# A bidirectional mLSTM encoder: an early mask, forward k weighted on ScalarE and VectorE, and another order of the pools

## The chip, the core and the metric

One core of a Trainium2 chip runs the whole kernel. The metric is the device time of one execution in microseconds (us), the median of the runs. The engines are TensorE (PE in the profile; PEld is its weight load), VectorE (DVE), ScalarE (ACT), GpSimd (POOL), and the queue SP, whose engine issues nearly all DMAs in order.

## The reference: what is computed

Two sequences, a prompt of 2048 tokens and a sample of 256, go through two layers: windowed attention, then a bidirectional mLSTM, each with gates and a residual, and a final RMS norm. All data is float32, width 1024. The change touches the mLSTM layer only, of 4 heads with 128 elements of q and k and 256 of v. Cut to what matters:

```python
def mlstm_chunkwise(q, k, v, ig, fg):
...
    logf = jax.nn.log_sigmoid(fg...)
    b = jnp.cumsum(logf, axis=-1)
    D = jnp.where(tri, b[..., :, None] - b[..., None, :] + igc[..., None, :], -jnp.inf)
    a = b_end[..., None] - b + igc
    m_loc = jnp.max(a, axis=-1)
    w = jnp.exp(a - m_loc[..., None])
    C_loc = jnp.einsum('bhcsk,bhcsv->bhckv', w[..., None] * kc, vc)
...
    def step(carry, inp):
        C, n, m = carry
        C_l, n_l, m_l, be = inp
        m_new = jnp.maximum(be + m, m_l)
        sp = jnp.exp(be + m - m_new)
        sl = jnp.exp(m_l - m_new)
        C_new = sp[..., None, None] * C + sl[..., None, None] * C_l
...
    P = jnp.exp(D - m_t[..., None]) * jnp.einsum('bhctk,bhcsk->bhcts', qc, kc)
    num = jnp.einsum('bhcts,bhcsv->bhctv', P, vc) + sc[..., None] * jnp.einsum('bhctk,bhckv->bhctv', qc, Cs)
    h = num / jnp.maximum(jnp.abs(den), jnp.exp(-m_t))[..., None]

def mlstm_mixer(xn, w_in, gate_bias, head_norm, w_out):
...
    h = h_f + h_b
    h = h * lax.rsqrt(jnp.mean(h * h, axis=-1, keepdims=True) + EPS)
...
    h = h * jax.nn.sigmoid(o) * jax.nn.silu(z)
    return h @ w_out
```

So a state C, 128 x 256 a head, runs forward over the chunks, and a second one backward; each chunk's output needs both.

## The kernel before, in words

The tokens lie in 18 tiles of 128, 16 of the prompt (one segment) and 2 of the sample (the other). Float32 products are made from parts: an operand is split into a high part (xhi, whi, kh, vh: a cast on ScalarE) and a low part (xlo, wlo, kl, v: a subtraction on VectorE), and three products, high x high, low x high and high x low, are summed in PSUM. The big projections go over pairs of tiles as Winograd products: seven products of half matrices instead of eight, lines 293 to 295, in the PSUM tiles pj, c and d. Lines 342 to 344 are a plain product of the first pair of a stage, lines 398 to 400 the last projection.

The mLSTM layer comes in four stages.

1. `mlstm_qkv` projects q, k, v and the gates' inputs and stores them in DRAM.
2. `gate_sums` turns the gates' inputs into scales for each tile and head. It is one serial chain of small steps: sums over a tile (pb, pe), a transpose (pu, uT), its maximum (um), a product that puts 72 maxima on one partition (pr, umr), then on VectorE the scan over the 18 tiles in both directions (lines 763 and 766, names rw, umr, be; each step needs the one before), an exponential (spr), products that spread the results to all partitions (pl), the weights of k (line 777), a scan within the tiles (msc, MT), and rows (nT, sT) that are stored in DRAM for later; em at line 797 is the last exponential. Its tiles are in the pool "gt".
3. `mlstm_gates_states` projects z and o, Winograd over nine pairs and two column halves. `use` (lines 866 to 880) takes a PSUM tile, adds the Winograd sum u where there is one (tile s), applies the Sigmoid into a tile e (line 872), multiplies (lines 874, 879) and stores to `go`. Meanwhile the backward state runs: `back_state` stores C to `Cb` and `state_update` makes cu products (line 828) from the parts of the weighted k and of v. The tiles e and s are in the pool "b2", k, v and C in "b2s".
4. `mlstm_core` runs forward. Generators for a tile are interleaved after the string ORDER: `weights` loads q, k (both transposed), rows and v, and makes E, the masked and exponentiated decay matrix times S = k q (S at line 919, mask cm added at line 926, exp at 928, times S at 929, parts Eh and El), and qs, the scaled q (line 933, on GpSimd); `core` makes num (line 948 from E and v, line 950 from the states and qs), the quotient hh, its sum of squares ss and the norm (lines 961 to 966); `update` weights k and updates the forward C; `back` transposes hh, splits it and projects it with w_mo (lines 398 to 400), and the final norm is stored to y.

What sets the order. Tile's scheduler lists the instructions of each engine ahead of time, and each engine then runs its list in order. Pools are opened and closed as the stages go, and a tile of a new pool waits for those tiles that held its bytes before. Raw loads from DRAM go through rings of slots: "rawx", "raww" (8 slots) and, in stage 3, "rawk".

In the compiled program the pools lie as follows (bytes in each partition). Before, b2 comes first: its three e and two s are at 126816 to 137056, which stage 2 does not use; b2s follows with kl, kh, v, vh and C at 137056 to 153536. The tiles of gate_sums are at 145120 to 155424. In the core, b3v's v parts are at 130912 to 139168.

The forward k's weighting is `weighted_k` (line 811): a raw load, one multiplication on GpSimd (line 817), a cast on ScalarE (818) and a subtraction on VectorE (819). The mask is loaded at the start of the core (line 894), the weights w_mo ahead of the loop over the tiles.

Of the kernel before, what the change touches and what calls it, by code (L numbers as in the profile page):

```python
# [11 lines left out]
F32 = mybir.dt.float32  # L12
F32R = mybir.dt.float32r
BF16 = mybir.dt.bfloat16
AF = mybir.ActivationFunctionType
ALU = mybir.AluOpType
# [4 lines left out]
D = 1024  # L21
# [6 lines left out]
MH, DQK, DV = 4, 128, 256  # L28
# [17 lines left out]
AORDER = "fffssssfsffffppsvppv"  # L46
AORDER1 = "fffssssfsffffppsvppv"
AORDER2 = "ssppsspvpv"
KX, WL = 0, 0
PH3, PL3 = (), ()  # L50
EA, ES, EQ = 2, 18, 0
ORDER = "cubwbubccucbcbuwubbbbbbw"
# [3 lines left out]
def seg_of(t):  # L56
    for s in SEGS:
        if s[0] <= t < s[1]:
            return s


class Trunk:
# [748 lines left out]
    def weighted_k(self, p, t, d, raw=()):  # L811

        nc = self.nc
        k = self.stage(self.k[t][:].rearrange("p h d -> p (h d)"), *raw).rearrange("p (h d) -> p h d", h=MH)
        lo = p.tile([128, MH, DQK], F32R, tag="kl", name="kl", bufs=1)
        hi = p.tile([128, MH, DQK], F32R, tag="kh", name="kh", bufs=1)
        nc.gpsimd.tensor_mul(k, k, self.w[:, d, t, :].unsqueeze(2).to_broadcast([128, MH, DQK]))
        nc.scalar.copy(hi[:], k)
        nc.vector.tensor_sub(lo[:], k, hi[:].bitcast(F32))
        return hi, lo  # L820
# [14 lines left out]
    def mlstm_gates_states(self):  # L835
        nc, tc, a = self.nc, self.tc, self.a
        with ExitStack() as st:
            pe = st.enter_context(tc.tile_pool(name="b2", bufs=2, reuse_waits="tile"))
            p = st.enter_context(tc.tile_pool(name="b2s", bufs=1, reuse_waits="tile"))
            ps = st.enter_context(tc.tile_pool(name="b2ps", bufs=1, space=PSUM, reuse_waits="tile"))  # L840
            prev = None

            ready = {}

            def operands(t):
                if t > 0 and t > seg_of(t)[0]:
                    ready[t] = self.weighted_k(p, t, 1, ("rawk",)), self.parts(p, self.v[t], "v", raw=("rawk",))

            def back_state(t):
                nonlocal prev  # L850
                s0, s1 = seg_of(t)
                if t < s1 - 1:
                    nc.sync.dma_start(self.Cb[t][:], prev[:])
                if t > s0:
                    if t == s1 - 1:
                        prev = p.tile([128, MH, VW], F32, tag="C", name="C", bufs=1)
                    self.state_update(ps, 1, t, *ready.pop(t), prev, prev, t == s1 - 1)
                operands(t - 1)

            operands(NT - 1)  # L860
            X = None
            for b in range(2):

                part = {}

                def use(t, h, o, u, b=b):
                    if u is not None:
                        s = pe.tile([128, 512], F32, tag="s", name="s", bufs=2)[:]
                        nc.vector.tensor_add(s, o, u)
                        o = s  # L870
                    e = pe.tile([128, 512], F32, tag="e", name="e", bufs=3)[:]
                    nc.scalar.activation(e, o, AF.Sigmoid)
                    if h == 0:
                        (nc.vector if u is None else nc.gpsimd).tensor_mul(e, e, o)  # L874
                    if t not in part:
                        part[t] = e
                        return
                    o = part.pop(t)
                    nc.gpsimd.tensor_mul(e, e, o)
                    nc.sync.dma_start(self.go[t][:, b * 512:(b + 1) * 512], e)  # L880

                X = self.winograd_pass(self.xn2T, a["w_oz"], b * 1024, self.g[:, 1], use, lambda n, pair: back_state(NT - 1 - b * len(PAIRS) - n),
                                       self.xn2T[:2] if b == 0 else None, X, True)


    def mlstm_core(self, y):
        nc, tc, a = self.nc, self.tc, self.a
        with ExitStack() as st:
            pool = lambda n, **k: st.enter_context(tc.tile_pool(name=n, bufs=2, reuse_waits="tile", **k))
            TRP, TRT = self.sps, "s"  # L890
            py, pm, pv, p, pe = pool("b3y", side="right"), pool("b3m"), pool("b3v"), pool("b3"), self.early
            ps = pool("b3ps", space=PSUM)
            cm = py.tile([128, 2, 128], F32, tag="cm", name="cm", bufs=1)
            nc.sync.dma_start(cm[:], a["causal"])
            w = []
            fg = pm.tile([128, D], F32, tag="fg", name="fg", bufs=1)
            nc.sync.dma_start(fg[:], a["final_g"].to_broadcast([128, D]))
            state = {0: None}
            W, H, R = {}, {}, {}

# [69 lines left out]
            def update(t):  # L970
                s0, s1 = seg_of(t)
                if t == s1 - 1:
                    state[t + 1] = None
                    return
                kw = self.weighted_k(py, t, 0, () if t < KX else ("raww",))
                yield
                C = p.tile([128, MH, VW], F32, tag="C", name="C", bufs=2)
                state[t + 1] = C
                for h in range(MH):
                    self.state_update(ps, 0, t, kw, W[t][3], state[t], C, t == s0, [h], 1)  # L980
                    yield

            def back(t):
                hh = H[t][:].rearrange("p h d -> p (h d)")
                xs = []
                for b in range(2):
                    tp = TRP.tile([128, 4, 128], F32, tag=TRT, name="tr", bufs=1)
                    for j in range(4):
                        nc.tensor.transpose(tp[:, j, :], hh[:, (b * 4 + j) * 128:(b * 4 + j + 1) * 128], self.ident[:])
                    xs += self.split(tp[:].rearrange("p c q -> p (c q)"))  # L990
                    yield
                x = [p.tile([128, 512], F32, tag="x", name="x", bufs=3)[:] for b in range(2)]
                for b in range(2):
                    nc.sync.dma_start(x[b], self.x2[t][:, b * 512:(b + 1) * 512])
                for b in range(2):
                    po = self.pj()
                    for qt in range(4):
                        self.project(po, xs, w[b], range(qt * 2, qt * 2 + 2))
                        if qt == 3:
                            nc.vector.tensor_add(x[b], x[b], po[:])  # L1000
                        yield
                rs = p.tile([128, 1], F32, tag="rs", name="rs", bufs=2)
                self.rms(p, x, rs[:])
                for b in range(2):
                    cols = slice(b * 512, (b + 1) * 512)
                    nc.vector.scalar_tensor_tensor(x[b], x[b], rs[:], fg[:, cols], ALU.mult, ALU.mult)
                    nc.sync.dma_start(y[t * 128:(t + 1) * 128, cols], x[b])
                yield

            self.free = deque(x for x in self.free if x[0] is self.wp)  # L1010
            for _ in weights(0):
                pass
            if not WL:
                w += self.load_w(a["w_mo"], [[512]] * 2, self.g[:, 2], PH3, PL3)
            for t in range(NT + 1):
                gens = {"c": core(t) if t < NT else iter(()), "u": update(t) if t < NT else iter(()),
                        "b": back(t - 1) if t > 0 else iter(()), "w": weights(t + 1) if t + 1 < NT else iter(())}
                for i, k in enumerate(ORDER):
                    if t == 0 and i == WL and WL:
                        w += self.load_w(a["w_mo"], [[512]] * 2, self.g[:, 2], PH3, PL3)  # L1020
                    next(gens[k], None)
                for g in gens.values():
                    for _ in g:
                        pass

    def run(self, y):
        nc, tc, a, ctx = self.nc, self.tc, self.a, self.ctx
        pjp = ctx.enter_context(tc.tile_pool(name="pjp", bufs=2, space=PSUM))
        self.pj = lambda: pjp.tile([128, 512], F32, tag="pj", name="pj")
        with tc.tile_pool(name="wy", bufs=1, side="right") as wy:  # L1030
# [3 lines left out]
            with ExitStack() as st:  # L1034
                right = lambda n, **k: st.enter_context(tc.tile_pool(name=n, bufs=1, side="right", reuse_waits="tile", **k))
# [9 lines left out]
                with tc.tile_pool(name="gps", bufs=1, space=PSUM, reuse_waits="tile") as self.gps:  # L1045
                    self.mlstm_qkv(first)
                    self.gate_sums()
                self.early = ctx.enter_context(tc.tile_pool(name="b3e", bufs=2, reuse_waits="tile"))
                self.mlstm_gates_states()
            self.xring = kept  # L1050
        self.mlstm_core(y)
# [81 lines left out]
```

## Time and profile before

| | |
|---|---|
| median of 3 runs (lowest, highest) | 2306.89 us (2303.06, 2307.14) |
| the profiled execution, its own time | 2307.11 us |
| its span on the core | 2305.0 us |
| mean granted TensorE clock in the span | 0.986 |
| busy: TensorE, weight loads, VectorE | 2217.8, 1763.9, 1505.6 us |
| busy: ScalarE, GpSimd | 1136.4, 464.1 us |

The times in the views are microseconds from the span's start. Stage 3's plain product ends at 1515.2, its last Winograd product at 1886.5; the core takes the rest. A row of a timeline has the start, the length, the engine, the line, the operation with its output and inputs, the shapes, how many instructions it stands for, and in brackets how long the engine was idle before it and what ended that. Matmuls overlap: one of 512 columns is listed with 0.39 us, but the next starts 0.23 us later. A row of groups has the busy time of all, the mean of one in ns, and the idle time ahead of them.

### The profile page before, as it was taken

How to read it: one execution, taken by the hardware profiler on the slowest of the kernel's cores; microseconds unless marked ns; L12 is line 12 of the kernel's file. 1: busy time of each engine (PE TensorE's matmuls, PEld its weight loads, DVE VectorE, ACT ScalarE, POOL GpSimd, SP SyncE). 2: the span in 40 equal slices, each digit the busy share in tenths (PEclk: the TensorE clock that was granted, in tenths of full speed). 3: DMA queues.
4: the chain of work that ended last, by engine and by line, in shares of the span. 5: the costliest groups of instructions: out<-in, count | busy, mean ns of one | idle time of the engine just before them, and what ended most of it. 6: DMA issues, size and time to landing. Idle time of an engine off the chain costs nothing. (4 is left out here: it accounts for less than half of the span.)

```text
span 2305.0 us, 33121 instructions
## 1 busy us (share of the span) xinstructions
PE 2217.8 (96%) x11102; PEld 1763.9 (77%) x11102; DVE 1505.6 (65%) x3303; ACT 1136.4 (49%) x2565; POOL 464.1 (20%) x392
## 2 busy tenths in 40 slices
PE   8999999999899999999999999999999977999998
PEld 7767676767567887788788899978878866888887
DVE  7565656565887779668656422386697576777784
ACT  6454545454764335557534411365464455454453
POOL 3211121211001222332000000022232243333320
PEclk9999999999999999999999999999999997999999
DMA  7111111111225447657655622356576565665641
GB/s 266 48 39 49 39 48 39 49 38 40 92 65 197 150 159 237 214 197 267 217 175 183 228 92 92 124 197 196 187 252 211 182 229 194 203 195 197 210 161 69
DMA packets 181802, 347.40 MB, mean 151 GB/s; under 512 B 20064, under 2 KB 22912, under 8 KB 181632
## 3 DMA queue, kind: packets, MB, share of 16 engines
q1 hardware_dynamic: 181488, 345.27, 45.0%
q8 instruction: 88, 1.44, 0.3%
q14 instruction: 82, 0.67, 0.1%
q10 hardware_dynamic: 144, 0.01, 0.0%
HBM read 247.93 MB, written 97.28 MB: 150 GB/s over the span
## 5 line engine op out<-in xcount | busy, mean ns | idle before, releaser
L398 PE MATMUL pj<-whi,xhi 128*128 128x512 f32 (+2 forms) x1152 | 433.6, 377 | 9.1 <-ACT whi L168 5.6
L123 ACT CAST xhi<-rawx 128x512 fp32r<-128x512 f32 x372 | 228.5, 618 | 418.4 <-PE pj L399 108.5
L400 PE MATMUL pj<-whi,xlo 128*128 128x512 f32 (+2 forms) x1152 | 423.2, 372 | 8.3 <-DVE xlo L124 8.3
L399 PE MATMUL pj<-wlo,xhi 128*128 128x512 f32 (+2 forms) x1152 | 426.3, 370 | 0.0
L124 DVE TENSOR_TENSOR xlo<-rawx,xhi 128x512 fp32r<-128x512 f32 x338 | 249.5, 743 | 106.7 <-ACT xhi L123 94.9
L400 PEld LDWEIGHTS pj<-whi,xlo 128*128 128x128 f32 x1152 | 218.0, 189 | 52.3 <-DVE xlo L124 11.4
L398 PEld LDWEIGHTS pj<-whi,xhi 128*128 128x128 f32 x1152 | 217.7, 189 | 51.3 <-issue 8.8
L399 PEld LDWEIGHTS pj<-wlo,xhi 128*128 128x128 f32 x1152 | 217.9, 189 | 36.6 <-issue 2.4
L536 ACT ACTIVATE Sm<-Sm,nm 128x384 f32<-128x384 f32 (+1 forms) x288 | 167.0, 581 | 95.0 <-DVE nm L530 88.6
L293 PE MATMUL pj<-whi,xhi 128*128 128x512 f32 x480 | 192.4, 401 | 2.7 <-DVE e L874 1.3
L294 PE MATMUL pj<-wlo,xhi 128*128 128x512 f32 x480 | 191.5, 399 | 0.4 <-DVE wlo L191 0.4
L295 PE MATMUL pj<-whi,xlo 128*128 128x512 f32 x480 | 191.3, 399 | 0.0
L525 DVE CUSTOM_DVE_ANT_0 Sm<-s,mask 128x384 f32<-128x384 f32 (+1 forms) x272 | 136.0, 530 | 72.1 <-PE s L523 69.0
L549 PE MATMUL ptp<-ident,Sm 128*128 128x128 f32 x800 | 135.3, 280 | 9.8 <-DVE PT L552 6.4
L549 PEld LDWEIGHTS ptp<-ident,Sm 128*128 128x128 f32 x800 | 94.6, 141 | 54.3 <-ACT Sm L536 19.0
L293 PE MATMUL c<-whi,xhi 128*128 128x512 f32 x320 | 127.5, 399 | 2.9 <-ACT whi L190 2.9
L293 PE MATMUL d<-whi,xhi 128*128 128x512 f32 x320 | 128.1, 400 | 1.4 <-DVE x L640 1.4
L294 PE MATMUL c<-wlo,xhi 128*128 128x512 f32 x320 | 127.1, 397 | 0.7 <-DVE wlo L191 0.7
L295 PE MATMUL c<-whi,xlo 128*128 128x512 f32 x320 | 127.0, 397 | 0.0
L294 PE MATMUL d<-wlo,xhi 128*128 128x512 f32 x320 | 126.4, 395 | 0.0
L295 PE MATMUL d<-whi,xlo 128*128 128x512 f32 x320 | 126.3, 395 | 0.0
L522 PE MATMUL s<-KH,Q 128*128 128x384 f32 (+1 forms) x288 | 106.0, 379 | 10.2 <-DVE mx L525 4.6
(242 smaller groups left out, 4650.9 us busy)
## 6 DMA issues: line engine op xcount, KB each, us to landing
rawx<-xn2T SPq DMA_DIRECT2D x128, 256.0 KB, 3.6
x<-x SPq DMA_DIRECT2D x108, 256.0 KB, 3.9
rawx<-xT SPq DMA_DIRECT2D x72, 256.0 KB, 3.0
raww<-w_oz SPq DMA_DIRECT2D x64, 256.0 KB, 4.8
rawx<-xsum SPq DMA_DIRECT2D x64, 256.0 KB, 3.0
raww<-w_qkvg SPq DMA_DIRECT2D x40, 256.0 KB, 4.3
v<-v SPq DMA_DIRECT2D x18, 516.0 KB, 3.8
rawx<-v SPq DMA_DIRECT2D x36, 258.0 KB, 2.8
```

Source lines behind the costliest of these rows:

```text
L123: nc.scalar.copy(hi[:], src)
L124: (eng or nc.vector).tensor_sub(lo[:], src, hi[:].bitcast(F32))
L293: nc.tensor.matmul(o, xh, wh, start=i == 0 and not more, stop=False, skip_group_check=more)
L294: nc.tensor.matmul(o, xh, wl, start=False, stop=False, skip_group_check=more)
L295: nc.tensor.matmul(o, xl, wh, start=False, stop=i == 3, skip_group_check=more)
L398: nc.tensor.matmul(o[:, :n], xh, wh, start=kt == 0, stop=False)
L399: nc.tensor.matmul(o[:, :n], xh, wl, start=False, stop=False)
L400: nc.tensor.matmul(o[:, :n], xl, wh, start=False, stop=kt == KT - 1)
L522: nc.tensor.matmul(S[:, :nk, :], q, KH[:, g, win, :], start=True, stop=False)
L525: nc.vector.tensor_tensor_reduce(Sm[:, :nk], S[:, :nk], mask[:, t % 3, win, :], 1.0, MASKED, ALU.add, ALU.max, mx[:, c:c + 1])
L536: nc.scalar.activation(Sg[c][:, :nk], Sg[c][:, :nk], AF.Exp, bias=nm[:, c:c + 1], scale=HD ** -0.5, accum_out=rs[:, c:c + 1])
L549: nc.tensor.transpose(tp[:, c, :], Ss[g][c][:, j, :], self.ident[:])
```

## The change

Four edits, in words:

1. The mask cm is a tile of the pool "b3e" (`self.early`), which is open over stages 3 and 4, and its load is issued ahead of `mlstm_gates_states`.
2. `weighted_k` for the forward direction (d == 0) has, for each of the four heads, a copy with a scale on ScalarE into the high part and a fused multiply and subtract on VectorE into the low one. GpSimd does nothing there. Its raw loads have a ring of their own, two slots taken from raww's eight. The switch KX, which was 0, is gone.
3. The pools are opened in another order: b2s before b2 in stage 3, b3v before b3m in the core, and the x tiles move from "b3" to "b3m". In the compiled program b2s is then at 127840 to 144320, e at 144320 to 150464 and s at 150464 to 154560, and the core's v parts are at 127840 to 144352, on the bytes of b2s.
4. w_mo is loaded inside the loop, at tile 0, and `issue_after` puts what ScalarE does for it behind the last Sigmoid of stage 3; the load of final_g follows it.

```diff
-KX, WL = 0, 0
+WL = 0
...
+        if d == 0:
+            for h in range(MH):
+                wk = self.w[:, d, t, h:h + 1]
+                nc.scalar.activation(hi[:, h], k[:, h], AF.Copy, scale=wk)
+                nc.vector.scalar_tensor_tensor(lo[:, h], k[:, h], wk, hi[:, h].bitcast(F32), ALU.mult, ALU.subtract)
+            return hi, lo
...
+            p = st.enter_context(tc.tile_pool(name="b2s", bufs=1, reuse_waits="tile"))
             pe = st.enter_context(tc.tile_pool(name="b2", bufs=2, reuse_waits="tile"))
-            p = st.enter_context(tc.tile_pool(name="b2s", bufs=1, reuse_waits="tile"))
...
-                    nc.scalar.activation(e, o, AF.Sigmoid)
+                    self.gated = nc.scalar.activation(e, o, AF.Sigmoid)
...
-            py, pm, pv, p, pe = pool("b3y", side="right"), pool("b3m"), pool("b3v"), pool("b3"), self.early
+            py, pv, pm, p, pe = pool("b3y", side="right"), pool("b3v"), pool("b3m"), pool("b3"), self.early
...
-            cm = py.tile([128, 2, 128], F32, tag="cm", name="cm", bufs=1)
-            nc.sync.dma_start(cm[:], a["causal"])
+            cm = self.cm
             w = []
+            ring = self.rings["raww"]
+            self.rings["rawk"] = deque(ring.pop() for _ in range(2))
...
-                kw = self.weighted_k(py, t, 0, () if t < KX else ("raww",))
+                kw = self.weighted_k(py, t, 0, ("rawk",))
...
-                x = [p.tile([128, 512], F32, tag="x", name="x", bufs=3)[:] for b in range(2)]
+                x = [pm.tile([128, 512], F32, tag="x", name="x", bufs=3)[:] for b in range(2)]
...
-            if not WL:
-                w += self.load_w(a["w_mo"], [[512]] * 2, self.g[:, 2], PH3, PL3)
...
-                    if t == 0 and i == WL and WL:
-                        w += self.load_w(a["w_mo"], [[512]] * 2, self.g[:, 2], PH3, PL3)
+                    if t == 0 and i == WL:
+
+                        with tc.issue_after(self.gated.ins):
+                            w += self.load_w(a["w_mo"], [[512]] * 2, self.g[:, 2], PH3, PL3)
+                        nc.sync.dma_start(fg[:], a["final_g"].to_broadcast([128, D]))
...
+                self.cm = self.early.tile([128, 2, 128], F32, tag="cm", name="cm", bufs=1)
+                nc.sync.dma_start(self.cm[:], a["causal"])
                 self.mlstm_gates_states()
```

Lines behind `weighted_k` have numbers that are six higher in the changed kernel (872 is 878 there, 919 is 925, 948 is 954).

The edits move instructions. TensorE where stage 2 ends and stage 3 begins, before: the last products of the plain pair (c, lines 342 to 344), then the first of the Winograd pair (pj, lines 293 to 295).

```order
L342 MATMUL c<-whi,xhi 128x512
L343 MATMUL c<-wlo,xhi 128x512
L344 MATMUL c<-whi,xlo 128x512
L293 MATMUL pj<-whi,xhi 128x512
L294 MATMUL pj<-wlo,xhi 128x512
L295 MATMUL pj<-whi,xlo 128x512
```

The same place in the changed kernel. s is the core's S of tile 0; pr, pl, pm and pM belong to gate_sums, cu to the backward state, of which only the first three of nine are shown (they differ in no name from the rest).

```order
L344 MATMUL c<-whi,xlo 128x512
L925 MATMUL s<-qT,kT 128x128 x4
L750 MATMUL pr<-ident,um 1x72 x2
L775 MATMUL pl_15014<-rw,ones 128x144
L772 MATMUL pl<-spr,ones 128x144
L782 MATMUL pm<-ones,rw 72x1 x2
L795 MATMUL pM<-ident,MT 128x72 x2
L834 MATMUL cu<-vh,kh 128x258
L834 MATMUL cu<-v,kh 128x258
L834 MATMUL cu<-vh,kl 128x258
...
L293 MATMUL pj<-whi,xhi 128x512
```

All of gate_sums' products after pu, which before stand among the Winograd products, now stand ahead of the first of them, and so do nine cu products and tile 0's S.

ScalarE at the same place in the changed kernel: spr, the weights of k (line 777), the rows (sT), em (line 797), a copy of the backward state's first C, and then the first Sigmoids (line 878), on the plain pair's pj.

```order
L770 ACTIVATE spr<-spr 1x144
L777 ACTIVATE scr<-scr 128x144
L790 ACTIVATE sT<-MT,msc 72x128
L824 CAST kh<-rawk 128x512
L790 ACTIVATE sT<-MT,msc 72x128
L797 ACTIVATE scr<-scr 128x144
L836 COPY C<-cu 128x258
L878 ACT_TABLE_LOAD
L878 ACTIVATE e<-pj 128x512 x2
L878 ACTIVATE e<-c 128x512
```

Before, the first Sigmoid stands ahead of all of these, between conversions of w_oz.

ScalarE where stage 3 ends and the core begins, before: the last Sigmoids (e), the last conversions of w_mo (whi, line 168), the exponentials and the high parts of E, and the high parts of v (vh, line 807, two casts for a tile).

```order
L872 ACTIVATE e<-s 128x512
L818 CAST kh<-raww 128x512
L168 ACTIVATE whi<-raww,g 128x512
L928 ACT_TABLE_LOAD
L928 ACTIVATE E<-E,scr 128x128 x8
L930 CAST Eh<-E 128x512
L872 ACT_TABLE_LOAD
L872 ACTIVATE e<-s 128x512
...
L928 ACTIVATE E<-E,scr 128x128 x4
L807 CAST vh<-rawx 128x516 x4
```

The same place in the changed kernel, from the last Sigmoid but one on.

```order
L936 CAST Eh<-E 128x512 x2
L820 ACTIVATE kh<-rawk,scr 128x128 x4
L878 ACTIVATE e<-s 128x512
L168 ACTIVATE whi<-raww,g 128x512 x6
L934 ACT_TABLE_LOAD
L934 ACTIVATE E<-E,scr 128x128 x8
L936 CAST Eh<-E 128x512
L807 CAST vh<-rawx 128x516 x4
L936 CAST Eh<-E 128x512
L934 ACTIVATE E<-E,scr 128x128 x3
L168 ACTIVATE whi<-raww,g 128x512
L934 ACTIVATE E<-E,scr 128x128
```

The exponentials of tile 0 have moved into stage 3 (its Eh stands here ahead of the last Sigmoid), vh comes one tile's E earlier, and all sixteen conversions of w_mo, which before were done by about here, stand behind the last Sigmoid: six ahead of tile 1's E, ten between what follows.

More of the change, by code (lines that the diff above doesn't have):

```diff
@@ L890, in mlstm_core @@
             TRP, TRT = self.sps, "s"
-            py, pm, pv, p, pe = pool("b3y", side="right"), pool("b3m"), pool("b3v"), pool("b3"), self.early
+            py, pv, pm, p, pe = pool("b3y", side="right"), pool("b3v"), pool("b3m"), pool("b3"), self.early
             ps = pool("b3ps", space=PSUM)
-            cm = py.tile([128, 2, 128], F32, tag="cm", name="cm", bufs=1)
-            nc.sync.dma_start(cm[:], a["causal"])
+            cm = self.cm
             w = []
+            ring = self.rings["raww"]
+            self.rings["rawk"] = deque(ring.pop() for _ in range(2))
             fg = pm.tile([128, D], F32, tag="fg", name="fg", bufs=1)
-            nc.sync.dma_start(fg[:], a["final_g"].to_broadcast([128, D]))
             state = {0: None}
```

## The prediction

> **What bounds the kernel now.** I read the page first, then a table of windows, then the waits of TensorE by stretch, and last the timelines around the two places that the change touches. The page's first line gives the span; the profiled execution took 2307.11 us, so 2.1 us lie around it, and it stands 0.2 us above the median of 2306.89, so I correct nothing.
>
> ```profile
> span 2305.0 us, 33121 instructions
> ```
>
> The windows (first the time and TensorE's busy time, then weight loads, VectorE, ScalarE, GpSimd; then the granted clock, the DMA share, GB/s):
>
> ```profile
> 1516.00:1526.00 10.00, 7.17 (x34) 5.39 (x32) 7.73 (x14) 5.19 (x11) 6.27 (x2) 0.95 0.34 116
> 1526.00:1532.00 6.00, 5.75 (x13) 4.23 (x14) 5.95 (x31) 2.13 (x4) 0.83 (x1) 0.51 0.86 266
> 1600.00:1880.00 280.00, 277.50 (x1271) 227.04 (x1271) 199.40 (x309) 138.50 (x238) 74.94 (x51) 1.00 0.62 203
> 1890.00:1900.00 10.00, 2.05 (x8) 1.78 (x8) 8.17 (x7) 6.64 (x13) 8.86 (x7) 0.51 1.01 362
> 1900.00:1910.00 10.00, 0.00 (x0) 0.00 (x0) 4.86 (x7) 5.49 (x16) 5.44 (x4) 0.50 0.90 322
> 1910.00:1920.00 10.00, 7.95 (x28) 6.67 (x29) 6.25 (x12) 7.26 (x23) 4.23 (x3) 0.50 0.74 228
> 1920.00:1930.00 10.00, 8.08 (x34) 7.07 (x33) 5.05 (x15) 4.44 (x14) 2.07 (x2) 0.67 0.48 152
> 2050.00:2250.00 200.00, 196.20 (x1091) 169.42 (x1090) 155.61 (x379) 105.40 (x295) 63.45 (x55) 1.00 0.58 191
> ```
>
> TensorE is the bound nearly everywhere: 277.5 of 280 us in the backward states, 196.2 of 200 in the forward core. Any time that it loses before 1880 therefore comes out at the end, and nothing makes it up. It has two holes that this change can reach: a small one while the gate sums run (1516 to 1532), and a big one between the states and the core (1886 to 1930). The waits, in turn for 1510 to 1570, 1886 to 1945 and from 1945 to the end (who waits, for whom, us in total, times, longest):
>
> ```profile
> PE c L293 <- ACT whi L190: 2.9, 1, 2.9
> PE num L948 <- ACT vh L807: 11.6, 1, 11.6
> PE s L919 <- DVE E L929: 10.0, 1, 10.0
> PE pj L400 <- DVE xlo L124: 8.3, 7, 1.9
> ```
>
> **The gate sums: a new wait.** The pool order moves the gate outputs e and s from bytes that the projection stage had left long before onto the gate sums' own tiles. The plain pair's first outputs sit in the PSUM tiles pj, and the Sigmoid that empties them writes e; so pj now stays full until the gate sums let go, and the first winograd product, which needs a pj and came right behind the plain pair, waits:
>
> ```profile
> 1515.21 0.40 PE L344 MATMUL c<-whi,xlo 128*128 128x512 f32 x1
> 1515.45 0.39 PE L293 MATMUL pj<-whi,xhi 128*128 128x512 f32 x1
> ```
>
> In the order of after, the chain's small products (pr, pl, pm, pM) and nine cu stand between these two, and on ScalarE the Sigmoid stands behind every exponential of the chain. TensorE now waits out a serial scan that before was slipped between winograd products. When does it restart? From before's VectorE and ScalarE:
>
> ```profile
> 1521.46 0.41 DVE L747 TENSOR_REDUCE um<-uT 72x2 f32<-72x256 f32 x1
> 1528.51 0.29 DVE L752 COPY umr<-pr 1x144 f32<-1x144 f32 x1
> 1537.48 0.26 DVE L766 TENSOR_TENSOR rw<-rw,be 1x4 f32<-1x4 f32 x2
> 1537.66 0.25 DVE L763 TENSOR_TENSOR rw<-umr,rw 1x4 f32<-1x4 f32 x2
> ```
> ```profile
> 1524.88 0.60 ACT L872 ACTIVATE e<-c 128x512 f32<-128x512 f32 x1 [4.56 <-POOL e L879]
> ```
> ```profile
> L766 DVE TENSOR_TENSOR rw<-rw,be 1x4 f32<-1x4 f32 x32 | 5.1, 181 | 0.0
> L763 DVE TENSOR_TENSOR rw<-umr,rw 1x4 f32<-1x4 f32 x36 | 4.5, 146 | 0.0
> ```
>
> um ends at 1521.9; umr came only at 1528.5, because a Sigmoid held ScalarE for 4.6 us and a weight conversion behind it held VectorE. In after no Sigmoid stands there. With four operations of 0.65 (the size of e times pj below), umr and one wlo, the scan starts near 1525.0. It has 32 + 36 = 68 steps; undisturbed, two starts lie 0.18 apart, and some 14 overlap at half that: 6.1 us, until 1531.1. From there to a free pj:
>
> ```profile
> L872 ACT ACT_TABLE_LOAD x3 | 3.8, 1283 | 0.2 <-DVE s L869 0.2
> L872 ACT ACTIVATE e<-pj 128x512 f32<-128x512 f32 x3 | 1.8, 599 | 0.0
> L818 ACT CAST kh<-rawk 128x512 fp32r<-128x512 f32 x1 | 0.6, 617 | 0.0
> L777 ACT ACTIVATE scr<-scr 128x144 f32<-128x144 f32 x1 | 0.3, 324 | 0.3 <-DVE scr L776 0.3
> ```
> ```profile
> 1551.34 1.04 POOL L817 TENSOR_TENSOR rawk<-rawk,scr 128x512 f32<-128x512 f32 x1 [1.20 <-ACT scr L777]
> ```
> ```profile
> L874 DVE TENSOR_TENSOR e<-e,pj 128x512 f32<-128x512 f32 x3 | 2.0, 678 | 0.9 <-ACT e L872 0.9
> ```
>
> Three exponentials of 0.32, two VectorE steps like umr of 0.29, backward k on GpSimd 1.04, its cast 0.62, the table switch 1.28, Sigmoid 0.60, e times pj 0.68: 5.8 us. The small products, the first cu, the copy of C behind it and some ten handovers make it about 8.0, from 6 to 10. TensorE restarts near 1539.1, 23.7 us late. Then it is slow: after the 2.8 us without work before 1526 the clock stood at 0.51 through the next 6 us, in which half the work, 2.9 us, was lost. I charge the same: 26.6. The Trainium skill, "TensorE: Matmul & The Clock Gate", Part 1, gives some 3.4 us of sustained work until the clock is full, as an estimate 1.7 us lost, by which the forecast would be 1.2 us lower; the row of 1526 to 1532 shows the longer one, so the sum keeps 2.9.
>
> What comes off: about 1 us for the nine cu already done (0.12 each, half a product's pitch), and what before lost here and after does not lose again:
>
> ```profile
> L293 PE MATMUL pj<-whi,xhi 128*128 128x512 f32 x28 | 12.0, 429 | 0.2 <-ACT u L305 0.2
> L293 PE MATMUL c<-whi,xhi 128*128 128x512 f32 x16 | 6.7, 419 | 2.9 <-ACT whi L190 2.9
> ```
>
> From 1515.4 to 1566 these rows, the same for d, and L294 and L295 alike, are 3 x (28 + 16 + 16) = 180 products. At the pitch of the two starts above, 0.23, they need 41.8 of 50.6 us: 8.8 lost, on whi, half clock and small products. Net 26.6 - 1.0 - 8.8 = **+16.8 us**. Bounds: +13 (a chain of 6, um 1.8 us earlier) to +21 (umr as late as before). Queued behind the Sigmoids are xhi and u on ScalarE, behind e times pj the E of tile 0 on VectorE, which waits for a DMA. TensorE has 24 products, 11 us at half clock, before it needs those: nothing, but up to 5 us if that cover is too short.
>
> **Between states and core: the gain.** The last winograd product starts at 1886.17; its end, 1886.5, is T0 here.
>
> ```profile
> 1886.17 0.40 PE L295 MATMUL d<-whi,xlo 128*128 128x512 f32 x1
> 1896.54 2.05 PE L919 MATMUL s<-qT,kT 128*128 128x128 f32 x8 [9.96 <-DVE E L929]
> 1910.15 0.58 PE L948 MATMUL num<-vh,Eh 128*128 128x258 f32 x1 [11.57 <-ACT vh L807]
> 1916.15 2.09 PE L950 MATMUL num<-Cb,qs 128*128 128x258 f32 x4 [0.53 <-POOL qs L933]
> 1935.98 0.50 PE L398 MATMUL pj<-whi,xhi 128*128 128x512 f32 x1
> ```
> ```profile
> 1890.92 2.65 DVE L926 TENSOR_TENSOR E<-E,cm 128x512 f32<-128x512 f32 x2 [2.46 <-DMA cm<-causal]
> ```
> ```profile
> 1908.31 1.28 ACT L928 ACTIVATE E<-E,scr 128x128 f32<-128x128 f32 x4 [3.55 <-POOL E L926]
> ```
> ```profile
> 1914.83 1.27 POOL L933 TENSOR_TENSOR qs<-qT,qs 128x512 f32<-128x512 f32 x1 [1.72 <-DMA qs<-rows]
> ```
> ```profile
> raww<-w_mo SPq DMA_DIRECT2D x16, 256.0 KB, 3.8
> ```
>
> Three waits follow each other: the mask's DMA held E; the third tile's E held ScalarE, since GpSimd was late with its mask; behind it stood vh, and num waited until T0 + 23.7. After, the mask is there, tile 0's E is finished inside the states, and ScalarE has six whi (0.7 each, casts like kh with a scale), a table load, E of tile 1 (eight of 0.32), Eh and vh: 4.2 + 1.3 + 2.6 + 0.6 + 0.6 = 9.3. With E's own DMA, num starts at T0 + 12 to 13: -10.7. Three things eat of that. Ten whi more lie between the exponentials and hh, 7 us of ScalarE that before was done by then. qs of tile 0 now stands behind 7.3 MB on SP's queue (Cb, qT, kT, E, go and six w_mo, with the sizes in the issue rows), which at the 362 GB/s of the 1890 row is 20 us, so num<-Cb,qs starts at T0 + 23 against T0 + 29.7: a gain of 6.7. And the first L398, at T0 + 49.5 before, needs w_mo's last part. I take **-7**, from -1 to -11; the row that decides is qs's wait for its DMA.
>
> **The steady core.** Per tile GpSimd loses 1.04, ScalarE has four scaled copies (like the exponentials, 4 x 0.32) for a cast of 0.62, VectorE four fused operations of 128 columns for one subtraction. Their price is not in the trace; the nearest row is a fused one of 256:
>
> ```profile
> 1919.11 0.48 DVE L957 SCALAR_TENSOR_TENSOR hh<-num,r,hh 128x256 f32<-128x256 f32 x1 [0.28 <-ACT hh L956]
> ```
>
> So between 4 x 0.24 and 4 x 0.48, against a subtraction of 0.7: +0.3 to +1.2 us of VectorE a tile, which at 155.6 of 200 us has room, as TensorE has not. The 8.3 us of TensorE waiting for xlo can grow or shrink by some of it: 0, from -3 to +3. The x tiles' new pool and final_g's later load meet no wait of this list: 0. cm's load joins SP's queue ahead of the gate sums, among weight loads that are needed only when TensorE restarts: 0, and at most its few tenths of issue if those were late.
>
> **The sum.** 2307.1 + 16.8 - 7 + 0 = **2316.9 us**.
>
> **The rivals.**
>
> *The gain does not come, 2323* (0.17). The ten whi hold hh, and with it PSUM and the first L398, as the exponentials held vh before: the hole only changes its owner. For it: ScalarE is busy for 19.4 of the 30 us from 1890 without them. Against: at 0.7 each they fit into the 10.6 us left. 2307.1 + 16.8 - 1 = 2322.9.
>
> *Faster, 2301* (0.13). GpSimd's queue, not the DMAs, is what all the core's waits hang on: with 16 multiplications gone, qs and ss come early, the 11.6 us for vh go wholly (-10.7) and so do the 8.3 for xlo, while the scan's stall comes out at its low end: 2307.1 + 13 - 10.7 - 8.3 = 2301.1. It decides from 18 us of gain in the core on. For it: E's 3.55 from GpSimd. Against: qs waited for a DMA, and GpSimd is 63 of 200 us busy.
>
> *Nothing comes of the stall, or both cancel, within 0.2%* (0.15). If the order did not bind (the Sigmoids free pj while the scan runs), there would be nothing to lose; the tiles' shared bytes speak against it. Cancelling: +13 - 11 + 0 = 2309.
>
> **How the numbers follow.** My forecast has 0.55; the three rivals 0.17, 0.13 and 0.15. Beyond 0.2%, 4.6 us, about what a measurement of this kernel can tell from no change, slower has 0.55 + 0.17 = 0.72, faster 0.13, the same 0.15. The range: the forecast's own is 13 - 11 - 3 to 21 - 1 + 3, 2306 to 2330, but both ends need three terms at once. I take 2303 to 2325, which leaves out the faster rival and the uppermost corner.
>
> **What would show it.** Right: a hole of 20 to 25 us on TensorE from 1515, ended by e times pj, the scan's rows dense, half clock behind it; T0 near 1903; num at 12 to 14 us after T0, its Cb part held by qs's DMA; the first L398 some 42 us after T0. Wrong: winograd products within the chain, which would break the gate term; or a first L398 under 38 us or over 48 us after T0, which would break the second. A core whose waits for xlo change by over 3 us would break the third.

## The result and the profile after

The changed kernel takes 2323.98 us, the kernel before 2305.64 us (medians of six runs each; three of the six gave the 2306.89 of the table above). The ratio is 1.0086, with an interval of 1.0073 to 1.0098: the change makes the kernel slower by some 0.86%, 20 us by the ratio and 18 by the medians. Forecast was slower, to 2316.9 us: the direction was right, the size half of what came, and of the three terms one failed.

The page of the changed kernel and, from its windows (the time and TensorE's busy time, weight loads, VectorE, ScalarE, GpSimd, then the granted clock, DMA share, GB/s), the two stretches that the prediction spoke of:

```profile
span 2321.6 us, 33211 instructions
```
```profile
1516.00:1526.00 10.00, 4.32 (x26) 3.26 (x24) 9.60 (x20) 6.85 (x11) 0.00 (x0) 0.82 0.76 249
1526.00:1532.00 6.00, 0.01 (x1) 0.04 (x1) 5.97 (x68) 0.00 (x0) 0.00 (x0) 0.50 0.44 153
1532.00:1540.00 8.00, 5.06 (x19) 3.94 (x19) 3.38 (x11) 4.27 (x9) 1.11 (x2) 0.50 0.30 86
1540.00:1546.00 6.00, 5.06 (x12) 4.00 (x13) 2.90 (x4) 5.56 (x11) 2.25 (x2) 0.50 0.23 85
1546.00:1554.00 8.00, 8.00 (x36) 6.54 (x36) 5.18 (x9) 7.01 (x15) 1.28 (x1) 0.98 0.36 130
...
1910.00:1920.00 10.00, 2.08 (x8) 1.89 (x9) 8.78 (x15) 6.89 (x16) 3.81 (x2) 0.50 1.03 377
1920.00:1930.00 10.00, 5.36 (x21) 4.38 (x20) 6.16 (x11) 8.01 (x21) 1.27 (x1) 0.67 1.05 395
1930.00:1940.00 10.00, 7.02 (x40) 5.67 (x39) 8.53 (x29) 8.44 (x25) 3.05 (x3) 0.90 0.76 256
1940.00:1950.00 10.00, 7.60 (x38) 6.57 (x38) 7.48 (x22) 5.32 (x18) 3.68 (x3) 0.83 0.37 119
```

From 1526 to 1532 TensorE does nothing, VectorE runs the scan, ScalarE and GpSimd stand. From 1910 to 1950 ScalarE is busy for 28.7 us of 40, and in no window is TensorE full. TensorE's waits by stretch, first the gate sums, then the start of the core, then the rest:

```profile
PE pl L775 <- DVE rw L763: 8.7, 1, 8.7
PE pr L750 <- DVE um L747: 3.0, 1, 3.0
PE pj L293 <- DVE e L880: 1.6, 1, 1.6
```
```profile
PE num L954 <- ACT vh L807: 8.7, 1, 8.7
PE cu L834 <- ACT C L836: 4.6, 3, 2.1
PE s L925 <- DMA kT<-kT: 4.5, 1, 4.5
PE cu L834 <- ACT kh L820: 3.5, 1, 3.5
```
```profile
PE pj L400 <- DVE xlo L124: 11.7, 12, 2.9
```

TensorE's timeline through the hole: the plain pair's last product, the chain's small products, and the Winograd product that ends it.

```profile
1518.40 0.39 PE L344 MATMUL c<-whi,xlo 128*128 128x512 f32 x1
...
1522.64 0.64 PE L750 MATMUL pr<-ident,um 72*1 72x72 f32 x4 [2.97 <-DVE um L747]
1531.99 0.81 PE L775 MATMUL pl<-rw,ones 1*128 1x144 f32 x2 [8.71 <-DVE rw L763]
...
1538.90 0.42 PE L834 MATMUL cu<-vh,kl 128*128 128x258 f32 x1
1540.94 0.79 PE L293 MATMUL pj<-whi,xhi 128*128 128x512 f32 x1 [1.62 <-DVE e L880]
```

ScalarE and VectorE at the hole's end: the last exponential (em), the copy of C, the switch of the table, the Sigmoids, and e times pj, which frees the PSUM tile.

```profile
1536.75 0.32 ACT L797 ACTIVATE scr<-scr 128x144 f32<-128x144 f32 x1 [0.60 <-DVE scr L796]
1537.88 0.37 ACT L836 COPY C<-cu 128x258 f32<-128x258 f32 x1 [0.81 <-PE cu L834]
1538.27 1.28 ACT L878 ACT_TABLE_LOAD   x1
1539.57 1.09 ACT L878 ACTIVATE e<-pj 128x512 f32<-128x512 f32 x2
```
```profile
1540.20 1.29 DVE L880 TENSOR_TENSOR e<-e,pj 128x512 f32<-128x512 f32 x2 [3.48 <-ACT e L878]
```

This is the chain as forecast: from 1518.6 to 1540.9 TensorE waits out the gate sums, 22.3 us (22.5 from start to start, as the holes below are counted), and the clock then stays at 0.50 until 1546.2, when the products come 0.23 apart again.

**Where the time went.** One profile of each kernel is cut at three points: the start of the plain pair's last product, T0 (the end of the last Winograd product, at 1903.1 in the changed kernel), and the first product with w_mo (line 398).

| | before | changed | forecast |
|---|---|---|---|
| plain pair to T0 | 371.4 | 384.7 | +16.8 |
| T0 to line 398 | 49.4 | 46.8 | -7 |
| line 398 to the end | 369.0 | 371.6 | 0 |

The first row lost 13.3 us, T0 to the end nothing (418.4 in both): the gain of 7 did not come. At the end of the plain pair the changed kernel's profile was already 3.2 us later. Half of that stands at the gate sums' first exponential (line 726, at 1498.5 against 1496.8), ahead of which each engine has the same list in both kernels, so two executions differ by this much without any edit; in the thirteen profiles of this study the plain pair's last product starts anywhere from 1512.9 to 1519.5. That is why the terms below rest on many profiles and on the timed runs.

### The profile page after: what moved, and what is told of

It is laid out like the page before. It is cut to its first block, busy times and chain, and to the rows that moved or that the text cites. A ratio compares the mean times of both kernels' runs of the same rounds, so it can differ in the third digit from the quotient of the medians.

```text
span 2321.6 us, 33211 instructions
## 1 busy us (share of the span) xinstructions
PE 2222.6 (96%) x11102; PEld 1768.0 (76%) x11102; DVE 1497.2 (64%) x3351; ACT 1139.6 (49%) x2608; POOL 442.4 (19%) x376
## 5 line engine op out<-in xcount | busy, mean ns | idle before, releaser
L400 PE MATMUL pj<-whi,xlo 128*128 128x512 f32 (+2 forms) x1152 | 423.9, 373 | 11.7 <-DVE xlo L124 11.7
L400 PEld LDWEIGHTS pj<-whi,xlo 128*128 128x128 f32 x1152 | 218.2, 189 | 57.3 <-DVE xlo L124 16.8
```

The costliest lines, as they stand in the source:

```text
L400: nc.tensor.matmul(o[:, :n], xl, wh, start=False, stop=kt == KT - 1)
```

## The experiments

Theory A: the hole at the gate sums is the loss, and it comes from where the pools lie. Rival B: the hole costs little, and the late conversions of w_mo are the loss. Theories of the core came after. Runs of before spread over up to three quarters of a per cent, so the ratios with their intervals count. For each kernel the table has this ratio and, from its one profile, three stretches in us.

| | ratio to before (interval) | plain pair to T0 | T0 to line 398 | T0 to end |
|---|---|---|---|---|
| before | 1 | 371.4 | 49.4 | 418.4 |
| changed | 1.0086 (1.0073 to 1.0098) | 384.7 | 46.8 | 418.4 |
| swap_alone | 1.0067 (1.0052 to 1.0082) | 388.2 | 48.0 | 411.5 |
| after_pools_back | 1.0003 (0.9990 to 1.0016) | 367.2 | 45.7 | 416.8 |
| after_wmo_early | 1.0076 (1.0060 to 1.0091) | 388.5 | 43.8 | 412.8 |
| after_both_back | 0.9976 (0.9965 to 0.9988) | 372.1 | 40.8 | 411.0 |
| gate_tiles_low | 1.0082 (1.0068 to 1.0096) | 389.2 | 46.7 | 414.0 |
| pools_touch | 1.0099 (1.0078 to 1.0121) | 388.5 | 46.3 | 419.8 |
| mask_alone | 0.9984 (0.9975 to 0.9994) | 369.9 | 43.3 | 407.8 |
| k_alone | 0.9987 (0.9975 to 0.9999) | 370.5 | 43.1 | 412.5 |
| mask_and_k | 1.0005 (0.9992 to 1.0018) | 371.1 | 44.8 | 416.8 |
| no_order_for_wmo | 0.9969 (0.9957 to 0.9981) | 366.5 | 40.7 | 411.4 |
| changed_no_order | 1.0069 (1.0051 to 1.0088) | 388.4 | 41.6 | 412.1 |

The last column has to be read with care. before, swap_alone, gate_tiles_low and pools_touch have no edit in the core, and yet their T0 to the end runs from 411.5 to 419.8; their T0 to line 398 lies closer together, 46.3 to 49.4, 47.6 on average.

**swap_alone**: before, with the two pools of stage 3 in the new order.

```diff
+            p = st.enter_context(tc.tile_pool(name="b2s", bufs=1, reuse_waits="tile"))
             pe = st.enter_context(tc.tile_pool(name="b2", bufs=2, reuse_waits="tile"))
-            p = st.enter_context(tc.tile_pool(name="b2s", bufs=1, reuse_waits="tile"))
```

> The kernel before with one edit of the four: b2s is opened ahead of b2, so that the gate outputs e and s lie on gate_sums' tiles. Theory A (the stall on e is the loss): TensorE has a hole of 20 to 24 us behind the plain pair, ended by e times pj, and the time is 13 to 18 us above before, 2319 to 2324. Rival B (the loss comes from the core, where sixteen conversions of w_mo and their loads stand behind the last Sigmoid; the hole is made up for by conversions done ahead): within 3 us of before, 2303 to 2309.

Measured: 2317.24 us against 2301.98, 0.67% or 15 us slower, with the same hole and the same wait in it. The waits of its TensorE:

```profile
PE pl L775 <- DVE rw L763: 9.5, 1, 9.5
...
PE pj L293 <- DVE e L874: 1.6, 1, 1.6
```

A holds: one swapped line brings 15 of the 20 us.

**after_pools_back**: the changed kernel with the same two lines back in the old order (the diff above, reversed).

> The changed kernel with b2 opened ahead of b2s again, as before, and the other edits kept. Theory A: no hole behind the plain pair; 13 to 18 us off, 2306 to 2311. Rival B: 2320 to 2326, as the changed kernel, since w_mo is still late.

Measured: 2302.41 us, the same as before within 0.16%. Its TensorE goes on at once behind the plain pair:

```profile
1516.23 0.39 PE L344 MATMUL c<-whi,xlo 128*128 128x512 f32 x1
1516.45 0.40 PE L293 MATMUL pj<-whi,xhi 128*128 128x512 f32 x1
```

A holds from the other side. But without the hole the other edits leave nothing, so the core's 7 us are still missing.

**after_wmo_early** and **after_both_back**: the changed kernel, and the one with the pools back, each with w_mo and final_g loaded ahead of the loop as before.

```diff
             for _ in weights(0):
                 pass
+            w += self.load_w(a["w_mo"], [[512]] * 2, self.g[:, 2], PH3, PL3)
...
-                    if t == 0 and i == WL:
-
-                        with tc.issue_after(self.gated.ins):
-                            w += self.load_w(a["w_mo"], [[512]] * 2, self.g[:, 2], PH3, PL3)
```

> The changed kernel with w_mo and final_g loaded ahead of the core's loop again, with no order put on ScalarE; the pools stay as changed. Theory A: the hole stays; from the end of the states (T0) to the first product with w_mo it is 3 to 6 us shorter than in the changed kernel (46.9 us there), and the time is 2318 to 2321. Rival B: 2305 to 2309, the whole loss gone.

> The changed kernel with both undone: b2 ahead of b2s, w_mo ahead of the loop; what is left is the early mask, forward k without GpSimd and the core's pools. Theory A with a gain in the core: 2300 to 2304, below before. Rival B: 2305 to 2309, the same as with w_mo undone alone. If the early mask and the k weighting bring nothing either, A gives 2304 to 2308.

Measured: 1.0076 with the hole, 0.9976 without. T0 to line 398 became 3.0 us shorter with the hole (43.8 for 46.8), 4.9 without (40.8 for 45.7). With w_mo early, the rest of the change gains 0.24% without the hole. B is out: undoing w_mo alone left the loss in place.

**no_order_for_wmo**: pools back, w_mo still inside the loop and with six slots, but without the order on ScalarE.

```diff
-                        with tc.issue_after(self.gated.ins):
+                        if True:
                             w += self.load_w(a["w_mo"], [[512]] * 2, self.g[:, 2], PH3, PL3)
```

> The changed kernel with b2 ahead of b2s, and w_mo loaded inside the loop but without the order that puts ScalarE's part behind the last Sigmoid. If that order costs the 6 us between the two kernels without the hole, this one is at their faster end, about 0.25% under before; if it is the later place in the program or the six slots, it stays within 0.1% of before.

Measured: 2296.93 us, ratio 0.9969, 0.34% under the same kernel with the order. So, without the hole, the order costs, and neither the later place in the program nor the six slots. It has the lowest ratio of this study, level with after_both_back within the intervals, and it beats both kernels.

**changed_no_order**: the changed kernel with this one edit.

> The changed kernel with all its pools, and only the order that puts w_mo's part of ScalarE behind the last Sigmoid taken away. If the hole at the gate sums and that order are two separate losses that add up, the hole stays (22 us) and the time is 0.2 to 0.35% below the changed kernel, a ratio to before of 1.005 to 1.0065. If the hole hides the order's cost, the ratio stays at 1.0075 or more.

Measured: 1.0069, between the two values that were expected, with a hole of 24.1 us. The interval overlaps that of the changed kernel, so the runs do not show that the two losses add up. In the profile T0 to line 398 is 41.6 us against 46.8: there the order costs with the hole too. But swap_alone, which has the hole and nothing else of the change, is at 1.0067: with the hole, the early mask, the k weighting and the core's pools show no gain in the timed runs (the intervals are 0.15 to 0.19% to each side), where without it they show 0.24 to 0.31%. Why is open.

**gate_tiles_low**: before, with the pools in the old order, and the gate sums' tiles pushed down onto e and s.

```diff
             nT = p.tile([n1, 2, 128], F32, tag="nT", name="nT")
+            gap = p.tile([128, 4480], F32, tag="gap", name="gap")
+            nc.vector.memset(gap[:1, :1], 0.0)
```

> The kernel before with its pool order kept, and an unused tile of 17920 bytes added at the end of the pool gt, so that gate_sums' tiles lie at 127200 to 137504, on the bytes of e and s. If shared bytes make the hole (theory A), it comes here too, without any change of the pool order: 20 to 26 us between the plain pair and the first Winograd product, and 12 to 22 us above before. If it was something else in the order of the pools, no hole, within 3 us of before. The gate sums' tiles also lie on the v tiles of the projection here, which can make the chain start a few us later.

Measured: 1.0082 and a hole of 24.4 us, from 1516.8 to 1541.2, at a c that a Sigmoid empties. The order of the pools is innocent by itself; what counts is what lies on what.

**pools_touch**: the same tile, of 2048 elements, at the start of gt instead. gate_sums' own tiles then lie as in before, and e lies clear of the whole pool.

> The kernel before with its pool order kept and an unused tile of 8192 bytes at the start of the pool gt, at 136928 to 145120. gate_sums' own tiles stay where they are, and e (126816 to 132960) shares no byte with gt; only the last 128 bytes of the second s tile do. If e waits for the tiles that lay on its own bytes, no hole, within 3 us of before. If pools that overlap anywhere wait as wholes, a hole of 20 us or more behind the plain pair, and 12 to 20 us above before.

Measured: 1.0099, and a hole again, from 1512.9 to 1537.0 at the first c. Its TensorE:

```profile
1520.52 0.64 PE L752 MATMUL pr<-ident,um 72*1 72x72 f32 x4 [5.27 <-DVE um L749]
1527.73 0.82 PE L777 MATMUL pl<-rw,ones 1*128 1x144 f32 x2 [6.57 <-DVE rw L765]
...
1536.98 0.80 PE L293 MATMUL c<-whi,xhi 128*128 128x512 f32 x1 [1.38 <-ACT e L874]
```

So e is held without sharing a byte with gt. That b2 and gt overlap anywhere, here in 128 bytes of a tile s, is enough for e to come behind the whole chain in ScalarE's list. (The same tile, cut so short that it shares no byte with b2, was not run.) Before, b2s overlapped gt, whose weighted k needs the chain's result anyway, and b2 did not.

**mask_alone**, **k_alone** and **mask_and_k**: before with one or both of these edits (k_alone with its ring of two slots, mask_and_k from raww), and nothing else.

```diff
+                self.cm = self.early.tile([128, 2, 128], F32, tag="cm", name="cm", bufs=1)
+                nc.sync.dma_start(self.cm[:], a["causal"])
                 self.mlstm_gates_states()
```
```diff
+        if d == 0:
+            for h in range(MH):
+                wk = self.w[:, d, t, h:h + 1]
+                nc.scalar.activation(hi[:, h], k[:, h], AF.Copy, scale=wk)
+                nc.vector.scalar_tensor_tensor(lo[:, h], k[:, h], wk, hi[:, h].bitcast(F32), ALU.mult, ALU.subtract)
+            return hi, lo
```

> The kernel before with the early mask alone. If the mask's wait is what starts the hole of the core (theory: the first cause in the row), the time from T0 to the end falls by 4 to 7 us, 5 us off in all. If GpSimd's weighting of k holds it all the same, within 2 us of before.

> The kernel before with forward k weighted on ScalarE and VectorE from a ring of its own, and nothing else. Theory: the mask still holds E, so 0 to 3 us off; GpSimd's wait for E of tile 2 is gone, the waits for xlo do not change. Rival: GpSimd's queue is what holds the core, 5 us or more off.

> The kernel before with the early mask and with forward k weighted on ScalarE and VectorE, from raww as before; no pool is moved in the core and w_mo stays ahead of the loop. If the two add up, 0.3% under before (0.16 and 0.13). If they remove the same wait, 0.15 to 0.2% under. Where it equals the version that has the core's pools too (0.24% under), the place of V brings nothing.

Measured: 0.16% and 0.13% off alone, with intervals that come down to 0.06% and 0.01%, and nothing together (0.9992 to 1.0018). mask_alone's gain lies between the two values that were expected, and its 407.8 us come from the fastest of its twelve runs. They don't add up here, but k's loads come from another ring in mask_and_k than in k_alone. That the two take away the same wait isn't shown, since together they should then have kept 0.15%. With the core's pools and k's ring besides (after_both_back) there is 0.24% again. The place of V and x or the ring thus matters once mask and k are in, but which of them, these runs don't tell: it stays open.

## Why the prediction was right and wrong

**The gate sums (+16.8): right.** The hole was forecast as 23.7 us and measured as 22.3. By its steps: the scan ran without a break, from 1525.8 to 1531.8, 6.1 us as forecast; from there to a free pj it took 9.1 us where I took 8.0 from a range of 6 to 10. Half clock: 12 products from 1540.94 to 1546.22 at 0.43 instead of 0.23, 2.5 us lost for 2.9. From the plain pair to T0, the six kernels with the hole need 387.9 us on average (384.7 to 389.2), the seven without it 369.8 (366.5 to 372.1): 18 us. Kernels that differ in the hole alone differ by 0.67 to 1.00% in the timed runs, 15 to 23 us; why it costs more in some is open. T0 near 1903 came as forecast (1903.1), but by luck: 3.2 us of it had been lost ahead of the hole. The nothing that I charged for the cover behind e times pj held: E waited 0.55 us for its DMA at 1542.0, and TensorE ran on without a wait.

One thing in it was wrong without harm: that "a tile of a new pool waits for those tiles that held its bytes before", as the section on the kernel has it. In pools_touch e stood behind the whole chain without sharing a byte with it.

**Between states and core (-7): wrong, 0 came.** The failed step reads: "I take -7, from -1 to -11; the row that decides is qs's wait for its DMA." The first half went roughly as forecast: num at T0 + 14.8 (forecast 12 to 13, before 23.6), 8.8 us earlier; num with Cb at T0 + 25.7 (forecast 23, before 29.6). But qs's DMA, the row that was to decide, did not hold this Cb part: GpSimd started on qs of tile 0 at T0 + 20.3 and was done 4 us ahead of it. What failed is the price of the ten later conversions: I had named them and let them cost less than 4 us. With them line 398 comes at T0 + 46.8, which is no earlier than the 46.3 to 49.4 of the kernels without an edit in the core. They are in ScalarE's order ahead of what TensorE waits for. ScalarE of the changed kernel, and TensorE's waits for it:

```profile
1923.70 2.56 ACT L168 ACTIVATE whi<-raww,g 128x512 fp32r<-128x512 f32 x4
1926.16 0.35 ACT L836 COPY C<-cu 128x258 f32<-128x258 f32 x1
...
1939.93 0.71 ACT L168 ACTIVATE whi<-raww,g 128x512 fp32r<-128x512 f32 x1
1940.55 0.45 ACT L962 ACTIVATE hh<-num,r 128x256 f32<-128x256 f32 x1
1940.90 1.26 ACT L820 ACTIVATE kh<-rawk,scr 128x128 fp32r<-128x128 f32 x4
```
```profile
1926.56 0.58 PE L834 MATMUL cu<-vh,kh 128*128 128x258 f32 x1 [2.10 <-ACT C L836]
...
1941.34 0.39 PE L834 MATMUL cu<-vh,kh 128*128 128x258 f32 x1 [3.52 <-ACT kh L820]
```

Four whi stand ahead of the copy of C for which cu waits 2.1 us, and others ahead of kh, for which it waits 3.5. The order holds loads as well. Six of the sixteen loads of w_mo are issued by 1747 and sit in the six slots; the other ten need slots that conversions free, and go out behind T0, where the prediction counted six. The queue SP and GpSimd in the changed kernel, then GpSimd in no_order_for_wmo:

```profile
1910.47 0.99 SPq L114 DMA_DIRECT2D raww<-w_mo  x2
...
1925.23 2.37 SPq L114 DMA_DIRECT2D raww<-w_mo  x4
```
```profile
1930.80 2.52 POOL L932 TENSOR_TENSOR E<-E,cm 128x512 f32<-128x512 f32 x2 [6.11 <-DMA raww<-w_mo]
```
```profile
1902.27 2.49 POOL L932 TENSOR_TENSOR E<-E,cm 128x512 f32<-128x512 f32 x2 [0.48 <-DMA E<-rows]
```

GpSimd's second E is at T0 + 27.7 with the order and at T0 + 20.9 without. How much of the order's cost goes by ScalarE's list and how much by the loads, no run tells apart. Without the order one conversion of w_mo is left after T0 and done before E of tile 1 comes, its loads are all issued before T0 (the last at 1877.1), and nothing of w_mo stands in the core's way. ScalarE and TensorE of no_order_for_wmo:

```profile
1884.76 0.71 ACT L168 ACTIVATE whi<-raww,g 128x512 fp32r<-128x512 f32 x1
...
1899.88 0.35 ACT L836 COPY C<-cu 128x258 f32<-128x258 f32 x1
1901.02 0.37 ACT L836 COPY C<-cu 128x258 f32<-128x258 f32 x1 [0.79 <-PE cu L834]
```
```profile
1896.98 0.58 PE L954 MATMUL num<-vh,Eh 128*128 128x258 f32 x1 [7.12 <-ACT vh L807]
...
1904.67 0.39 PE L834 MATMUL cu<-vh,kh 128*128 128x258 f32 x1 [0.63 <-ACT C L836]
...
1922.11 0.51 PE L398 MATMUL pj<-whi,xhi 128*128 128x512 f32 x1 [0.68 <-ACT xhi L123]
```

T0 is 1881.4 here. num starts at T0 + 15.6, hardly other than in the changed kernel, but line 398 comes at T0 + 40.7. From T0 to line 398, the four kernels with all the core's edits and without the order need 40.7 to 43.8, 41.7 on average, the two with it 45.7 and 46.8, and the four without an edit in the core 47.6: the order takes back 4.5 of the 5.9 us that the other edits bring there. In the timed runs it costs 0.34% without the hole, 8 us, clear of noise, and 0.17% with it, 4 us, which the intervals do not clear. The gain of 7 that I forecast for the whole core is seen in the timed runs only without the hole (0.31%). My sign for a failure of this term, a line 398 later than T0 + 48, was set too wide to see it. The rival of 0.17, "the gain does not come, 2323", is what happened, and by the ten conversions that it names; but it had them hold hh, and the waits are for C and kh.

**The steady core (0, from -3 to +3): within its bounds, +2.6 in the one profile.** TensorE's waits for xlo were 11.7 us instead of 8.3 in the changed kernel and 11.0 in after_pools_back, and 3.9 to 8.6 in nine kernels without the order, but 11.0 in mask_and_k and pools_touch too, of which the second has neither the order nor the k weighting. The k weighting itself did no harm there: k_alone waits 8.0. The price of the k weighting on VectorE came within its bounds from a wrong base: per tile the four fused operations took 1.95 us (0.53 each) in the changed kernel's core, and the one subtraction before took 1.36 where I had 0.7. From line 398 to the end the four kernels without an edit in the core need 363.5 to 373.5 us, so 2.6 us in one pair tell nothing, and I do not count this as settled.

**The sum.** 2307.1 + 16.8 - 7 = 2316.9. With the sizes measured, 2305.6 + 18 + 0 = 2323.6, against 2323.98; that they meet so closely is partly luck, since in the one pair of profiles the parts are 3.2 us ahead of the hole, 13.3 and 0. The faster rival (GpSimd holds the core) did not come: k_alone, with GpSimd free of forward k, gains 0.13%, 3 us and not 20, and TensorE still waits 4.5 us for vh and 11.2 for a DMA ahead of S in it. Nor did the third: the hole is there, and nothing cancels it.

## What to carry to other kernels

Ask of each pool, when it is moved or enlarged, which pool lay there last and when that one ends, not only which tile: here an overlap of 128 bytes was enough to put a serial chain of 20 us on the path. Work taken out of one engine's queue to make room there isn't hidden when it is put behind a fixed point; it stands in front of whatever comes next, it keeps the slots that later loads need, and what counts is who waits for those. Price each edit of a bundle alone on the chip: of this one, one swapped line cost 15 us or more and one order 8 where the hole did not cover it, and without both it is faster than before by 0.31%.

## What the runs showed of the hardware

The granted clock took long to come back. After the hole of 22 us it was 0.50 through 1540 to 1546, with TensorE at work without a break from 1540.9, and full from 1546.2 on: 5.3 us, like the 6 us of before behind a stall of 2.8. The Trainium skill, "TensorE: Matmul & The Clock Gate", Part 1, gives some 3.4 us of sustained work; the trace does not agree with that, and in this kernel 5.3 to 6 us are what to charge. Rows on one partition ran on VectorE at 0.18 us for a step and its successor in the changed kernel, with TensorE's clock at half, and in the rows of before from 1537.48 on, with TensorE's products 0.23 apart. The chain of 68 of them, when nothing stood between them, cost 6.1 us in the changed kernel and in pools_touch alike.
